# A two-layer hybrid trunk: the side steps' account, column strips and F32R logits

## The chip, the cores and the metric

The kernel runs on one core of a Trainium2 chip. The metric is the device time of one execution in microseconds (us): the median of several runs. Its engines are TensorE (PE in the profile; its weight loads are PEld), VectorE (DVE), ScalarE (ACT), GpSimd (POOL) and SyncE (SP).

## The reference, cut to what matters

Two layers over 256 tokens of width 2048. One input projection feeds four branches of width 512 (4 heads of 128): sparse attention with an indexer (A), retention (B), a gated linear recurrence (C) and attention into 256 memory tokens (M).

```python
def hybrid_layer(x, mem, ...):
    u = rms_norm(x, norm_g) @ w_in          # 2048 -> 15944 columns
    # A: rel = relu(q_idx . k_idx / 8); score = sum_h w_h rel_h; top 64 keys; softmax attention
    # B: rope(q), rope(k); (q . k) * decay; @ v; head norm
    # C: f = lb + (1 - lb) sigmoid(c_f); state = f * state + (1 - f) i; out = q . state; head norm
    # M: softmax(q . mk) @ mv, with mk, mv = mem @ w_mem_kv
    for n, (y, z) in enumerate(((y_a, a_z), (y_b, b_z), (y_c, c_z), (y_m, m_z))):
        merged = merged + sigmoid(gate_all[:, :, n]) * ((y * silu(z)) @ w_branch[n])
    return x + merged @ w_out
```

## The kernel before

**Products.** Weights stream from HBM in blocks of 512 rows by up to 512 columns (`gemm_plan`, `load`), four blocks ahead. Each half block is cut by `cut_piece` into a high part, a ScalarE copy to F32R (L247), and a low part, a VectorE subtraction (L248); four halves can be held (HL). `gemms` (L263) makes a product from three F32R matmuls (L286 to L288: high x high, high x low, low x high) for each 128 rows of the left side and each half of the tokens: twelve matmuls a half block, which leave the 256 tokens' results in PSUM. After each half block it calls `stream.pump` (L290), and then writes the next cut (L292).

**Side steps.** All that is not such a product (norms, rope, logits, softmax, the indexer's top-k, the recurrence's blocks, transposes) is written as Python generators, held as `Task` in `stream.tasks`. `pump` (L126) counts a tick (a half block of 512 columns is 1, narrower ones less) and steps the tasks in the order in which they were added, up to two steps (STEPS) a tick; a step that yields BLOCKED costs nothing. So each engine's instructions stand in an order that the program's writing fixes, and every engine runs its own in that order. `rest(n)` blocks a task until n ticks have gone by since it was reached; `bank` and `free` count two PSUM tiles for side products. `fold` transposes 32x32 blocks on VectorE and moves the blocks with 16 DMAs on POOL and SP, four a tick, then rests three ticks. `finish` (L136) is called where a product needs a task's result: it steps that task on with no product between, and counts ticks where nothing can move.

**The order of a layer.** Products: c_f and c_q, c_i, c_z, the indexer (256 and 328 columns), a_q, a_k, a_v, a_z, m_q, m_z, b_q, b_k, b_v, b_z; then four times, for branches C, A, M, B: the gate projection (8 ticks) and the branch product (2 ticks, L925), ahead of which `finish` takes the branch; then the output projection. Ahead of the first layer stand the memory's keys and values, whose left sides `memx` are split 8b - 4 ticks after the start (`split_later`).

**What the change touches.** `attend` (L426: logits at L439 in F32; memory without masks), `retention_scores` (L558: first key block at L562), `selection` (the indexer, L504: two heads side by side on rows 0 to 63 and 64 to 127), `hgrn_scores` (L652: groups of four column strips of 48 columns; L682: the last pair of levels, three strips of 96, 64 and 32 columns), `rope_t`, `branch_t` (transposes a branch and splits it, L303 and L304), `gate_path`. An F32 matmul of the program shows as two TensorE instructions.

Of the kernel before, what the change touches and what calls it, by code (L numbers as in the profile page):

```python
# [41 lines left out]
C_ID, C_D, C_COS, C_SIN, C_LEV = 0, 32, 32 + 1536, 32 + 1536 + 256, 32 + 1536 + 512  # L42
QUADS, FROM = (2, 8), (0, 1, 2, 0, 1, 0)
# [29 lines left out]
class Task:  # L73
    def __init__(self, steps):
        self.steps, self.done, self.value = steps, False, None

    def step(self):
        try:
            return next(self.steps) is not BLOCKED
        except StopIteration as e:  # L80
            self.done, self.value = True, e.value
            return True
# [7 lines left out]
GEN, HL, RAW = 18, 4, 4  # L90
MOVES, STEPS, BANKS, WARM = 4, 2, 2, 7


class Stream:
    def __init__(self):
        self.loaded = self.cut = self.used = self.ticks = self.idle = self.banks = 0
        self.owed = self.due = self.sent = 0
        self.raw, self.parts, self.tasks, self.moves = deque(), deque(), [], deque()
# [27 lines left out]
    def pump(self, part):  # L126
        self.tick(part)
        self.due = min(self.due + STEPS * part, STEPS)
        for t in list(self.tasks):
            if self.due < 1:  # L130
                break
            self.due -= t.step()
            if t.done:
                self.tasks.remove(t)
# [48 lines left out]
def trunk(ctx: ExitStack, tc: tile.TileContext, x, xt, memt, ng, qkg, hg, lbl, win, wmem, wbr, wout,  # L183
          cf, out):
    nc = tc.nc
    te, ve, ac, po, sy = nc.tensor, nc.vector, nc.scalar, nc.gpsimd, nc.sync
# [9 lines left out]
    def G(shape, name, dt=F32):  # L196
        return gen.tile(shape, dt, tag="g", name=name)
# [24 lines left out]
    stream = Stream()  # L222
# [23 lines left out]
    def cut_piece(hi, lo, r):  # L246
        ac.copy(hi, r)  # L247
        ve.tensor_sub(lo, r, hi.bitcast(F32))  # L248
# [110 lines left out]
    def transposed(src, name):  # L359
        u = yield from fold([((4, 2), src.rearrange("p t (h c) -> p h t c", h=4))], 8, name)  # L360
        return u.rearrange("p (h t) c -> p h (t c)", h=4)
# [12 lines left out]

    def normed_t(ps, rs, g, name):
        u = evac(ps, rs, name + "u")

        def turn():
            sq = G([128, 2, 512], name + "sq")
            ac.activation(sq, u, AF.Square)  # L380
            yield
            ss = SM(8, name + "ss")
            ve.reduce_sum(ss, sq.rearrange("p t (h d) -> p (t h) d", h=4), axis=AX.X)
            r = yield from rsq(ss, 8, 1.0 / HD, name)
            yield
            qn = u.rearrange("p t (h d) -> p (t h) d", h=4)
            ve.tensor_mul(qn, qn, bc(r, HD))
            yield
            pt = yield from transposed(u, name + "pt")
            ac.activation(pt, pt, AF.Copy, scale=g)  # L390
            return pt
        return turn()
# [10 lines left out]
    def branch_t(y, name):  # L403
        u = yield from transposed(y, name + "pt")
        return split(u, gen, "g", name)

    def head_norm(ps, zs, g, name):
        v = ps.rearrange("p (a d) -> p a d", a=8)
        zg = G([128, 2, 512], name + "zg")
        ve.tensor_tensor(zg, zs, g[:, None, :].to_broadcast([128, 2, W]), op=OP.mult)  # L410
        sq = G([128, 8, 128], name + "sq")
        ac.activation(sq, v, AF.Square)
        yield
        ss = SM(8, name + "ss")
        ve.reduce_sum(ss, sq, axis=AX.X)
        r = yield from rsq(ss, 8, 1.0 / HD, name)
        yield
        y1 = G([128, 8, 128], name + "y1")
        ve.tensor_mul(y1, v, bc(r, HD))
        stream.free()  # L420
        y = G([128, 2, 512], name + "y")
        ve.tensor_tensor(y, y1.rearrange("p (t h) d -> p t (h d)", t=2), zg, op=OP.mult)
        yield
        return (yield from branch_t(y, name))

    def attend(box, names, keys, name):  # L426
# [5 lines left out]
        y = G([128, 2, 512], name + "y")  # L432
        for t in range(2):
            nk = keys[t]
            nb = nk // 128
            yield from stream.bank()
            lg = PB(f"{name}lg{t}")[:, :4 * nk].rearrange("p (h s) -> p h s", h=4)
            for h in range(4):
                te.matmul(lg[:, h, :], qt[:, h, t * 128:t * 128 + 128], kt[:, h, :nk], start=True, stop=True)  # L439
# [13 lines left out]
            for h in range(4):  # L453
                ac.activation(p[:, h, :], lg[:, h, :], AF.Exp, bias=nm[:, h:h + 1], scale=ISQ,
                              accum_out=sm[:, h:h + 1])
            if masks is None:
                stream.free()
# [21 lines left out]
        return (yield from branch_t(y, name))  # L479

    def selection(qi0, qi1, name):
# [11 lines left out]
        for t in range(2):  # L493
# [3 lines left out]
            for g in range(8 // per):  # L497
# [3 lines left out]
                for h in range(g * per, g * per + per):  # L501
                    j = (h % 2) * (per // 2) + (h % per) // 2
                    q = slice((h % 2) * 64, (h % 2) * 64 + 64)
                    te.matmul(ps[:, j, :], qit[q, h // 2, t * 128:t * 128 + 128], kit[q, :nk],  # L504
                              start=True, stop=True)
# [20 lines left out]
    def rope_t(ps, rs, name):  # L526
        a = G([128, 2, 512], name + "a")
        b = G([128, 2, 512], name + "b")
        for t in range(2):
# [9 lines left out]
        ve.tensor_tensor(a, a, b, op=OP.add)  # L539

        def turn():
            yield
            return (yield from transposed(a, name + "pt"))
# [14 lines left out]
    def retention_scores(qt, kt, name):  # L558
        yield from stream.bank()
        p0 = PB(name + "s0").rearrange("p (h t) -> p h t", h=4)  # L560
        for h in range(4):
            te.matmul(p0[:, h, :], kt[:, h, 0:128], qt[:, h, :], start=True, stop=True)  # L562
# [13 lines left out]
    def hgrn_scores(uf, uq, lb, olb, name):  # L576
# [26 lines left out]

        strips = [slice(32 * i, 32 * i + 32) for i in range(4)]
# [75 lines left out]
        for g in range(8):  # L680
            for i, (c, w) in enumerate(((0, 96), (96, 64), (160, 32))):
                te.matmul(ps[strips[i], g, 128 - w:], kd[:, g // 2, (g % 2) * 128 + 32 * i:(g % 2) * 128 + 32 * i + 32],  # L682
                          vs[g // 4][:, g % 4, c:c + w], start=True, stop=True)
        for i, w in enumerate((96, 64, 32)):
            ac.copy(a[strips[i], :, 128 - w:], ps[strips[i], :, 128 - w:])
# [164 lines left out]
    for l in range(L):  # L850
# [8 lines left out]
        def mixed(scores, v, z, g, name):  # L859
            sc = yield from wait_for(box, key(scores))  # L860
            vt = yield from wait_for(box, key(v))
            zs = yield from wait_for(box, key(z))
            yield
            yield from stream.bank()
            return (yield from head_norm(mix_values(sc, vt, name), zs, g, name + "n"))
# [7 lines left out]
        early = []  # L873

# [12 lines left out]
        br[2] = stream.add(mixed("cs", "ci", "cz", hgs[:, 1, :], "c"))  # L887
# [8 lines left out]
        br[0] = stream.add(attend(box, [key(n) for n in ("aq", "ak", "av", "az", "ix")], (128, 256), "a"))  # L896
# [4 lines left out]
        br[3] = stream.add(attend(box, [key("mq"), f"mk{l}", f"mv{l}", key("mz"), None], (256, 256), "m"))  # L901
# [5 lines left out]
        br[1] = stream.add(mixed("bs", "bv", "bz", hgs[:, 0, :], "b"))  # L907
# [98 lines left out]
```

## Time and profile before

| | |
|---|---|
| median of 3 runs | 1866.32 us (1865.81 to 1867.09) |
| the profiled execution, its own time | 1866.38 us |
| its span, first to last instruction | 1864.4 us |
| instructions | 23441 |
| read from HBM | 353.60 MB |

The span lies 2.0 us below the profiled execution's own time. A busy time counts an instruction from its start to its end; matmuls overlap, so their pace is read from their starts.

### The profile page before, as it was taken

Reading aid. Unit: us, or ns where it says so; the run is one execution under the profiler, and the core shown is the slowest. Engines: PE = TensorE matmul, PEld = TensorE weight load, DVE = VectorE, ACT = ScalarE, POOL = GpSimd, SP = SyncE. Lnnn points to the kernel's source line nnn. Section 1 sums busy time; section 2 is a strip of 40 time slices with the busy share of each in tenths; the row PEclk is TensorE's granted clock in tenths of the full one; section 3 lists DMA queues with packets and bytes.
Section 4 is the critical chain, followed back from the end, with each engine's and each line's share of the span. In section 5 each row is a group of like instructions: output and inputs, shape, how many; then the busy total and the mean of one; then the engine's idle time right before and its main releaser. Section 6 shows DMA issues by size and latency. Waiting matters only on the chain.

```text
span 1864.4 us, 23441 instructions
## 1 busy us (share of the span) xinstructions
PE 1857.5 (100%) x8852; PEld 1548.7 (83%) x8852; DVE 1139.0 (61%) x1250; ACT 873.9 (47%) x1019; POOL 250.0 (13%) x405
## 2 busy tenths in 40 slices
PE   9999999999999999999999999999999999999999
PEld 7888888888888888888888888888888888888887
DVE  5655878675655555555566587867565555555554
ACT  5654554634444444444455454553444444444442
POOL 0022040241200000000021204024110000000000
PEclk9999999999999999999999999999999999999999
DMA  9775667686656565565686566668675656556563
GB/s 336 278 235 164 230 174 217 198 212 191 206 199 198 201 196 199 188 208 197 200 235 206 172 226 187 212 184 225 184 215 188 214 183 213 187 201 201 190 207 121
DMA packets 165952, 381.11 MB, mean 204 GB/s; under 512 B 111952, under 2 KB 112976, under 8 KB 125264
## 3 DMA queue, kind: packets, MB, share of 16 engines
q1 hardware_dynamic: 153408, 367.54, 60.8%
q0 software_dynamic: 12288, 11.95, 3.5%
q8 instruction: 69, 1.13, 0.2%
q14 instruction: 43, 0.35, 0.1%
q10 hardware_dynamic: 144, 0.13, 0.0%
HBM read 353.60 MB, written 2.10 MB: 191 GB/s over the span
## 4 chain that ended last, share of the span: by engine, by line
PE 99%; DMA 0%; DVE 0%; SPq 0%; ACT 0%; issue 0%
PE u L286 24%; PE u L287 24%; PE u L288 24%; PE wo L286 3%; PE wo L288 3%; PE bw L287 3%; PE bw L286 3%; PE bw L288 3%; PE wo L287 3%; PE mv L286 1%; PE mv L288 1%; PE mv L287 1%; PE mk L287 1%; PE mk L288 1%; PE mk L286 1%; PE mov L469 0%
## 5 line engine op out<-in xcount | busy, mean ns | idle before, releaser
L248 DVE TENSOR_TENSOR wlo<-raw,whi 128x1024 fp32r<-128x1024 f32 (+2 forms) x675 | 805.4, 1196 | 666.7 <-ACT whi L247 662.6
L247 ACT CAST whi<-raw 128x1024 fp32r<-128x1024 f32 (+2 forms) x675 | 696.0, 1032 | 918.1 <-PE u L288 697.3
L345 POOL DMA_DIRECT2D mgp<-mgpi x64 | 36.8, 583 | 797.8 <-ACT whi L247 589.8
L286 PE MATMUL u<-whi,x02h 128*128 128x512 f32 (+2 forms) x256 | 99.0, 387 | 0.0
L286 PE MATMUL u<-whi,x12h 128*128 128x512 f32 (+2 forms) x256 | 98.9, 387 | 0.0
L286 PE MATMUL u<-whi,x13h 128*128 128x512 f32 (+2 forms) x256 | 98.8, 386 | 0.0
L286 PE MATMUL u<-whi,x03h 128*128 128x512 f32 (+2 forms) x256 | 98.8, 386 | 0.0
L286 PE MATMUL u<-whi,x01h 128*128 128x512 f32 (+2 forms) x256 | 98.8, 386 | 0.0
L286 PE MATMUL u<-whi,x11h 128*128 128x512 f32 (+2 forms) x256 | 98.7, 386 | 0.0
L286 PE MATMUL u<-whi,x10h 128*128 128x512 f32 (+2 forms) x256 | 98.5, 385 | 0.0
L286 PE MATMUL u<-whi,x00h 128*128 128x512 f32 (+2 forms) x256 | 98.5, 385 | 0.0
L287 PE MATMUL u<-wlo,x02h 128*128 128x512 f32 (+2 forms) x256 | 98.2, 384 | 0.0
L287 PE MATMUL u<-wlo,x12h 128*128 128x512 f32 (+2 forms) x256 | 98.2, 384 | 0.0
L288 PE MATMUL u<-whi,x02l 128*128 128x512 f32 (+2 forms) x256 | 98.2, 384 | 0.0
L287 PE MATMUL u<-wlo,x03h 128*128 128x512 f32 (+2 forms) x256 | 98.2, 384 | 0.0
L287 PE MATMUL u<-wlo,x13h 128*128 128x512 f32 (+2 forms) x256 | 98.2, 384 | 0.0
L287 PE MATMUL u<-wlo,x11h 128*128 128x512 f32 (+2 forms) x256 | 98.2, 384 | 0.0
L287 PE MATMUL u<-wlo,x01h 128*128 128x512 f32 (+2 forms) x256 | 98.2, 384 | 0.0
L288 PE MATMUL u<-whi,x12l 128*128 128x512 f32 (+2 forms) x256 | 98.2, 384 | 0.0
L288 PE MATMUL u<-whi,x11l 128*128 128x512 f32 (+2 forms) x256 | 98.2, 384 | 0.0
L288 PE MATMUL u<-whi,x01l 128*128 128x512 f32 (+2 forms) x256 | 98.2, 384 | 0.0
L288 PE MATMUL u<-whi,x13l 128*128 128x512 f32 (+2 forms) x256 | 98.2, 384 | 0.0
(391 smaller groups left out, 3672.3 us busy)
## 6 DMA issues: line engine op xcount, KB each, us to landing
raw<-in_win SPq DMA_DIRECT2D x240, 1024.0 KB, 4.9
raw<-in_wbr SPq DMA_DIRECT2D x32, 1024.0 KB, 4.8
raw<-in_wout SPq DMA_DIRECT2D x32, 1024.0 KB, 4.8
raw<-in_wmem SPq DMA_DIRECT2D x12, 1024.0 KB, 5.2
raw<-in_win SPq DMA_DIRECT2D x8, 656.0 KB, 4.0
raw<-in_win SPq DMA_DIRECT2D x8, 512.0 KB, 4.0
raw<-in_wmem SPq DMA_DIRECT2D x5, 512.0 KB, 8.1
xr<-in_xt SPq DMA_DIRECT2D x4, 512.0 KB, 7.8
```

The lines of the kernel that those rows point to most:

```text
L247: ac.copy(hi, r)
L248: ve.tensor_sub(lo, r, hi.bitcast(F32))
L286: te.matmul(ps[t][:, u], ah[:, 2 * j + k, c], wh[:, k, u], start=first, stop=False)
L287: te.matmul(ps[t][:, u], ah[:, 2 * j + k, c], wl[:, k, u], start=False, stop=False)
L288: te.matmul(ps[t][:, u], al[:, 2 * j + k, c], wh[:, k, u], start=False, stop=last)
L345: q.dma_start(whole[b, :, a], inner[a, :, b])
```

## The change

**The account.** `Account` keeps a reckoned time for each engine; `Counted` and `Array` wrap the engines and add a formula's cost for each instruction written. `pump` stops stepping when VectorE or ScalarE are more than LATE (2500 ns) behind TensorE by it, and steps a task only when TensorE's time has reached the end of what the task's last step wrote, plus MARGIN (500 ns). **Later splits.** `branch_t` holds a branch's split until a given tick, counted from the tick at which the gates begin (`gates_at`). **F32R logits.** `halved` cuts an operand into two F32R halves (a ScalarE copy, a VectorE subtraction); `triple` makes a product of three F32R matmuls; memory logits and the retention's first block use it. **Strips.** The indexer's products go out as four strips of 32 output rows; the last pair's 96-wide piece is cut in 64 and 32, the latter on the fourth strip (`LAST`). Also: rope's second half of the tokens and its sum move into the task's steps, the exponentials are written in two steps, and GEN is 20 for 18.

```diff
@@ -40,6 +40,7 @@
...
 C_ID, C_D, C_COS, C_SIN, C_LEV = 0, 32, 32 + 1536, 32 + 1536 + 256, 32 + 1536 + 512
+LAST = ((0, 0, 0, 32, 64), (1, 1, 96, 64, 64), (2, 2, 160, 96, 32), (3, 0, 64, 96, 32))
 QUADS, FROM = (2, 8), (0, 1, 2, 0, 1, 0)
@@ -72,14 +73,76 @@
...
     def __init__(self, steps):
-        self.steps, self.done, self.value = steps, False, None
-
-    def step(self):
+        self.steps, self.done, self.value, self.ready = steps, False, None, 0.0
+    def step(self, account=None):
+        if account:
+            account.touched = 0.0
         try:
-            return next(self.steps) is not BLOCKED
+            moved = next(self.steps) is not BLOCKED
         except StopIteration as e:
-            self.done, self.value = True, e.value
-            return True
+            self.done, self.value, moved = True, e.value, True
+        if account and moved:
+            self.ready = account.touched + MARGIN
+        return moved
+class Account:
+    def __init__(self):
+        self.at, self.touched, self.table = dict(te=0.0, ve=0.0, ac=0.0, po=0.0), 0.0, None
+    def add(self, engine, cost, behind=()):
+        start = max([self.at["te"]] + [self.at[e] for e in behind] + [self.at[engine]])
+        self.at[engine] = start + cost
+        self.touched = max(self.touched, self.at[engine])
+    def late(self):
+        return max(self.at["ve"], self.at["ac"]) - self.at["te"]
+class Counted:
+    def __init__(self, engine, name, account):
+        self.engine, self.name, self.account = engine, name, account
+    def cost(self, op, args, kw):
+        n = max([int(np.prod(a.shape[1:])) for a in (*args, *kw.values()) if isinstance(a, bass.AP)] + [8])
+        if self.name == "po":
+            return 600 if op == "dma_start" else 1700 + n
+        if self.name == "ve":
+            return 155 + (1.4 if op == "copy_predicated" else 1.05) * n
+        func, table = kw.get("func", args[2] if op == "activation" and len(args) > 2 else None), 0
+        if func in (AF.Exp, AF.Sigmoid) and func != self.account.table:
+            self.account.table, table = func, 1300
+        return 215 + 0.8 * n + table + (200 if kw.get("accum_out") is not None else 0)
+    def __getattr__(self, op):
+        call = getattr(self.engine, op)
+        def counted(*args, **kw):
+            self.account.add(self.name, self.cost(op, args, kw))
+            return call(*args, **kw)
+        return counted
+class Array:
+    def __init__(self, engine, account):
+        self.engine, self.account = engine, account
+    def matmul(self, out, w, x, **kw):
+        n, k, m = int(np.prod(x.shape[1:])), w.shape[0], w.shape[1]
+        if x.dtype == F32R:
+            cost = (n + 32) / 2.4
+        else:
+            cost = (4 * n + 10) / 2.4 * (1.2 if k * m < 128 * 128 else 1.0) * k / 128 * m / 128
+        self.account.at["te"] += cost
+        self.account.touched = max(self.account.touched, self.account.at["te"])
+        return self.engine.matmul(out, w, x, **kw)
@@ -87,12 +150,14 @@
...
 HALVES = (slice(0, 256), slice(256, 512))
-GEN, HL, RAW = 18, 4, 4
+GEN, HL, RAW = 20, 4, 4
 MOVES, STEPS, BANKS, WARM = 4, 2, 2, 7
+MARGIN, LATE = 500.0, 2500.0
 class Stream:
-    def __init__(self):
+    def __init__(self, account):
+        self.account = account
         self.loaded = self.cut = self.used = self.ticks = self.idle = self.banks = 0
@@ -127,9 +192,10 @@
...
         for t in list(self.tasks):
-            if self.due < 1:
+            if self.due < 1 or self.account.late() > LATE:
                 break
-            self.due -= t.step()
+            if self.account.at["te"] >= t.ready:
+                self.due -= t.step(self.account)
             if t.done:
@@ -183,7 +249,9 @@
...
     nc = tc.nc
-    te, ve, ac, po, sy = nc.tensor, nc.vector, nc.scalar, nc.gpsimd, nc.sync
+    account = Account()
+    te, sy = Array(nc.tensor, account), nc.sync
+    ve, ac, po = (Counted(e, n, account) for e, n in ((nc.vector, "ve"), (nc.scalar, "ac"), (nc.gpsimd, "po")))
@@ -245,6 +313,7 @@
...
         ac.copy(hi, r)
+        account.at["ve"] = max(account.at["ve"], account.at["ac"])
         ve.tensor_sub(lo, r, hi.bitcast(F32))
@@ -372,6 +441,22 @@
...
+    def halved(src, name):
+        n = src.shape[2]
+        if n == 256:
+            hi, lo = G([128, 4, n], name + "hi", F32R), G([128, 4, n], name + "lo", F32R)
+        else:
+            both = G([128, 2, 4, n], name + "hl", F32R)
+            hi, lo = both[:, 0], both[:, 1]
+        ac.copy(hi, src)
+        yield
+        ve.tensor_sub(lo, src, hi.bitcast(F32))
+        return hi, lo
+    def triple(out, w, x):
+        for i, (a, b) in enumerate(((0, 0), (0, 1), (1, 0))):
+            te.matmul(out, w[a], x[b], start=i == 0, stop=i == 2)
@@ -400,11 +485,13 @@
...
-    def branch_t(y, name):
+    def branch_t(y, name, until):
         u = yield from transposed(y, name + "pt")
+        while stream.ticks < until:
+            yield BLOCKED
         return split(u, gen, "g", name)
-    def head_norm(ps, zs, g, name):
+    def head_norm(ps, zs, g, name, until):
         v = ps.rearrange("p (a d) -> p a d", a=8)
@@ -421,22 +508,31 @@
...
-        return (yield from branch_t(y, name))
-
-    def attend(box, names, keys, name):
+        return (yield from branch_t(y, name, until))
+    def attend(box, names, keys, name, until):
...
+        ks = None
...
+            if masks is None:
+                qs = yield from halved(qt[:, :, t * 128:t * 128 + 128], f"{name}q{t}")
+                if ks is None:
+                    ks = yield from halved(kt, name + "k")
+                yield from stream.rest(2)
...
-                te.matmul(lg[:, h, :], qt[:, h, t * 128:t * 128 + 128], kt[:, h, :nk], start=True, stop=True)
+                if masks is None:
+                    triple(lg[:, h, :], [u[:, h, :] for u in qs], [u[:, h, :] for u in ks])
+                else:
+                    te.matmul(lg[:, h, :], qt[:, h, t * 128:t * 128 + 128], kt[:, h, :nk], start=True, stop=True)
@@ -453,6 +549,8 @@
...
                               accum_out=sm[:, h:h + 1])
+                if h == 1:
+                    yield
             if masks is None:
@@ -476,7 +574,9 @@
...
         yield
-        return (yield from branch_t(y, name))
+        return (yield from branch_t(y, name, until))
+    strips = [slice(32 * i, 32 * i + 32) for i in range(4)]
@@ -498,11 +598,13 @@
...
                 ps = PB(f"{name}rp{t}{g}").rearrange("p (h s) -> p h s", h=per)
-                for h in range(g * per, g * per + per):
-                    j = (h % 2) * (per // 2) + (h % per) // 2
-                    q = slice((h % 2) * 64, (h % 2) * 64 + 64)
-                    te.matmul(ps[:, j, :], qit[q, h // 2, t * 128:t * 128 + 128], kit[q, :nk],
-                              start=True, stop=True)
+                for h in range(g * per, g * per + per, 2):
+                    for st in strips:
+                        for odd in range(2):
+                            q = slice(odd * 64, odd * 64 + 64)
+                            te.matmul(ps[st, odd * (per // 2) + (h % per) // 2, :],
+                                      qit[q, h // 2, t * 128 + st.start:t * 128 + st.stop], kit[q, :nk],
+                                      start=True, stop=True)
                 rl = G([128, per, nk], f"{name}rl{t}{g}")
@@ -526,7 +628,8 @@
...
         b = G([128, 2, 512], name + "b")
-        for t in range(2):
+        def rotate(t):
             pv = ps[:, t, :].rearrange("p (h d) -> p h d", h=4)
@@ -536,9 +639,13 @@
...
                                         st[:, :, lo:lo + 64], op0=OP.mult, op1=OP.mult)
-        ve.tensor_tensor(a, a, b, op=OP.add)
+        rotate(0)
         def turn():
+            rotate(1)
+            yield
+            ve.tensor_tensor(a, a, b, op=OP.add)
             yield
@@ -556,10 +663,13 @@
...
     def retention_scores(qt, kt, name):
+        ks = yield from halved(kt[:, :, 0:128], name + "k")
+        qs = yield from halved(qt, name + "q")
+        yield from stream.rest(2)
         yield from stream.bank()
...
         for h in range(4):
-            te.matmul(p0[:, h, :], kt[:, h, 0:128], qt[:, h, :], start=True, stop=True)
+            triple(p0[:, h, :], [u[:, h, :] for u in ks], [u[:, h, :] for u in qs])
         s0 = G([128, 4, 256], name + "s0s")
@@ -678,11 +786,11 @@
...
         for g in range(8):
-            for i, (c, w) in enumerate(((0, 96), (96, 64), (160, 32))):
-                te.matmul(ps[strips[i], g, 128 - w:], kd[:, g // 2, (g % 2) * 128 + 32 * i:(g % 2) * 128 + 32 * i + 32],
+            for to, i, c, t0, w in LAST:
+                te.matmul(ps[strips[to], g, t0:t0 + w], kd[:, g // 2, (g % 2) * 128 + 32 * i:(g % 2) * 128 + 32 * i + 32],
                           vs[g // 4][:, g % 4, c:c + w], start=True, stop=True)
-        for i, w in enumerate((96, 64, 32)):
-            ac.copy(a[strips[i], :, 128 - w:], ps[strips[i], :, 128 - w:])
+        for to, i, c, t0, w in LAST:
+            ac.copy(a[strips[i], :, t0:t0 + w], ps[strips[to], :, t0:t0 + w])
         stream.free()
@@ -856,13 +964,13 @@
...
-        def mixed(scores, v, z, g, name):
+        def mixed(scores, v, z, g, name, until):
             sc = yield from wait_for(box, key(scores))
...
             yield from stream.bank()
-            return (yield from head_norm(mix_values(sc, vt, name), zs, g, name + "n"))
+            return (yield from head_norm(mix_values(sc, vt, name), zs, g, name + "n", until))
@@ -871,6 +979,7 @@
...
         early = []
+        gates_at = stream.ticks + sum(n for c, n in CHUNKS[:16]) / 64
@@ -884,7 +993,7 @@
...
         stream.add(keep(key("cs"), hgrn_scores(uf, uq, lbv[:, l, :], olb[:, l, :], "c")))
-        br[2] = stream.add(mixed("cs", "ci", "cz", hgs[:, 1, :], "c"))
+        br[2] = stream.add(mixed("cs", "ci", "cz", hgs[:, 1, :], "c", gates_at - 2))
         box[key("ci")] = evac(proj(O_CI), rs, "ci")
@@ -893,18 +1002,18 @@
...
-        br[0] = stream.add(attend(box, [key(n) for n in ("aq", "ak", "av", "az", "ix")], (128, 256), "a"))
+        br[0] = stream.add(attend(box, [key(n) for n in ("aq", "ak", "av", "az", "ix")], (128, 256), "a", gates_at + 4))
...
-        br[3] = stream.add(attend(box, [key("mq"), f"mk{l}", f"mv{l}", key("mz"), None], (256, 256), "m"))
+        br[3] = stream.add(attend(box, [key("mq"), f"mk{l}", f"mv{l}", key("mz"), None], (256, 256), "m", gates_at + 12))
...
-        br[1] = stream.add(mixed("bs", "bv", "bz", hgs[:, 0, :], "b"))
+        br[1] = stream.add(mixed("bs", "bv", "bz", hgs[:, 0, :], "b", gates_at + 20))
...

```

## Rows read from the trace of the kernel before

**Rows 1.** The page's parts 1 (busy us, share, instructions) and 2 (granted clock).
```profile
PE 1857.5 (100%) x8852; PEld 1548.7 (83%) x8852; DVE 1139.0 (61%) x1250; ACT 873.9 (47%) x1019; POOL 250.0 (13%) x405
...
PEclk9999999999999999999999999999999999999999
```

**Rows 2.** TensorE's waits: who waited for whom, us in total, times, longest.
```profile
PE mk L286 <- ACT whi L247: 1.5, 1, 1.5
PE heat L709 <- DVE warm L706: 1.1, 1, 1.1
```

**Rows 3.** Timeline of TensorE, no side work: start us, us, engine, line, tiles, form.
```profile
900.02 0.39 PE L286 MATMUL wo<-whi,mg1h 128*128 128x512 f32 x1
...
902.74 0.39 PE L286 MATMUL wo<-whi,mg2h 128*128 128x512 f32 x1
```

**Rows 4.** Timeline of TensorE around a group of the memory logits.
```profile
370.13 0.39 PE L288 MATMUL u<-whi,x02l 128*128 128x512 f32 x1
370.36 1.89 PE L439 MATMUL mlg<-mk0pt,mqpt 128*128 128x256 f32 x8
371.90 0.58 PE L286 MATMUL u<-whi,x03h 128*128 128x512 f32 x1
372.31 0.40 PE L287 MATMUL u<-wlo,x03h 128*128 128x512 f32 x1
```

**Rows 5.** Timeline of TensorE in the 256-wide projection.
```profile
190.22 0.28 PE L288 MATMUL u<-whi,x02l 128*128 128x256 f32 x1
...
191.42 0.28 PE L286 MATMUL u<-whi,x03h 128*128 128x256 f32 x1
```

**Rows 6.** TensorE by line and form: count, busy us, mean ns, idle before.
```profile
L439 PE MATMUL mlg<-mk0pt,mqpt 128*128 128x256 f32 x16 | 3.8, 379 | 0.0
...
L562 PE MATMUL bs<-bqpt,bkpt 128*128 128x256 f32 x16 | 3.8, 379 | 0.0
...
L682 PE MATMUL cl<-cV,ck 128*32 128x96 f32 x32 | 3.0, 248 | 0.0
```

**Rows 7.** Timeline of TensorE around L682's group and the first of L652.
```profile
237.75 0.39 PE L288 MATMUL u<-whi,x00l 128*128 128x512 f32 x1
238.06 1.51 PE L682 MATMUL cl<-cV,ck 128*32 128x96 f32 x48
239.50 0.50 PE L286 MATMUL u<-whi,x01h 128*128 128x512 f32 x1
...
208.78 0.89 PE L652 MATMUL cl<-cV,ck 128*32 128x48 f32 x64
209.60 0.50 PE L286 MATMUL u<-whi,x00h 128*128 128x512 f32 x1
```

**Rows 8.** Timeline of TensorE around two of the indexer's groups.
```profile
270.52 1.16 PE L504 MATMUL ixrp<-ixkt,ixqt 64*128 64x128 f32 x16
271.62 0.50 PE L286 MATMUL u<-whi,x02h 128*128 128x512 f32 x1
...
296.32 1.13 PE L504 MATMUL ixrp<-ixkt,ixqt 64*128 64x256 f32 x8
297.39 0.50 PE L286 MATMUL u<-whi,x02h 128*128 128x512 f32 x1
```

**Rows 9.** Timelines of VectorE and of TensorE in the memory block.
```profile
42.69 1.22 DVE L304 TENSOR_TENSOR meml<-memr,memh 128x1024 fp32r<-128x1024 f32 x1
...
51.60 0.39 PE L288 MATMUL mk<-whi,meml 128*128 128x512 f32 x1
```

**Rows 10.** Timelines of VectorE and of TensorE after the rope of bq.
```profile
386.66 1.18 DVE L248 TENSOR_TENSOR wlo<-raw,whi 128x1024 fp32r<-128x1024 f32 x1
...
388.64 0.39 PE L287 MATMUL u<-wlo,x02h 128*128 128x512 f32 x1
```

**Rows 11.** Lines 303 and 922: count, ns min/median/max, first and last start.
```profile
L303 ACT CAST mh<-mpt x2: 1051/1052/1052, 502.7 to 1385.6; 128x1024 fp32r<-128x1024 f32 x2
...
L922 ACT ACTIVATE gate<-u,rs0r x32: 677/680/682, 478.2 to 886.8; 128x512 f32<-128x512 f32 x32
```

More of the change, by code (lines that the diff above doesn't have):

```diff
@@ L221, in trunk @@
     plan = gemm_plan(wmem, win, wbr, wout)
-    stream = Stream()
+    stream = Stream(account)
     def load(pieces=((0, 4),)):
@@ L602, in decayed @@
             return nt
-        strips = [slice(32 * i, 32 * i + 32) for i in range(4)]
         def eight(mask, *shape):
```

## The prediction

> **What bounds the kernel now.** I read the page's busy times first, then the waits of TensorE, then the timeline of single stretches. The page gives TensorE 1857.5 us of work in a span of 1864.4 us, and its granted clock is full in every slice; VectorE has 61% and ScalarE 47% [rows 1]. A modelled busy time can hide small gaps, so the waits and the starts have to agree with it. They do: the view has four waits of TensorE, all on the warm-up's line and on the first product's (mk), the longest two 1.5 and 1.1 us [rows 2]. In a stretch without side work twelve product steps of 128x512 start 2.72 us apart, 0.227 us each [rows 3]. I call these twelve steps, one half block of weights, a tick. So the span is a queue of TensorE work with no holes. Time can be gained only by work that TensorE no longer does, and lost only where a hole opens. SyncE's, VectorE's and ScalarE's time is worth nothing as long as it doesn't open one.
>
> **The logits in F32R** (`triple` in `attend` for memory and in `retention_scores` for the first key block). Today a group of four F32 products of 256 columns shows as eight instructions of TensorE. In the stretch of the memory logits the last product step ahead starts at 370.13 and the second one behind at 372.31, 2.18 us; two steps are 0.45, so the group costs 1.73 us [rows 4]. The new group has twelve F32R products of 256 columns. The half-width projection runs such products: ten of them start in 1.20 us, 0.12 us each [rows 5]. Twelve are 1.44 us, a gain of 0.29. The memory logits are four groups (two a layer: 16 instructions for one layer's keys) and the retention scores two (16 in both layers, same mean of 379 ns) [rows 6]: 6 x 0.29 = **1.74 us**. Bounds: if the long step behind the group (0.41 against 0.227) stayed, it would be 0.11 a group, 0.66 in all; more than 1.74 has no reason, since the QI steps already run without a gap.
> The new halves need ScalarE copies and VectorE subtractions: per layer two of 1024 elements and three of 512. At 1.22 us [rows 9] and 1.05 us [rows 11] for 1024 these are at most 6.1 and 5.3 us a layer, on engines with 39% and 53% idle. Cost on the path: zero, hidden under the products, because each triple rests two ticks (5.4 us) behind the last subtraction.
>
> **Four strips in the last pair.** The group of L682 runs three strips side by side, 96, 64 and 32 columns wide; from its first start to the next product step are 1.44 us. The group of L652, four strips of 48 columns, takes 0.82 us [rows 7]. With eight head groups and four passes of F32, the widest strip streams 8 x 4 x 96 = 3072 columns in the one and 1536 in the other: 0.62 us for 1536 columns, 0.40 ns a column. With 64 as the widest strip it is 2048 columns: 0.82 + 512 x 0.40 ns = 1.03 us, a gain of 0.41 a layer, **0.82 us**. Bounds: 0 (the fourth piece runs behind the first one in the same time as before) and 1.24 (as quick as L652). One more ScalarE copy a layer is hidden.
>
> **The indexer's strips.** Today two 64-row halves run side by side. The first query block has 16 instructions in 1.10 us from first start to the next product step, each part of the second 8 instructions in 1.07 us [rows 8]. Four pairs of 128 or two pairs of 256 are 2048 columns each, if the halves run side by side; by the line of L682 and L652 strips would take 1.03 us for as many columns. The gain is 0.07 twice and 0.04 four times, 0.30 at most. Eight pieces also start one after another, so I take **0.2 us**, between 0 and 0.30. No row has pieces that are cut in both directions; the loss if they don't run side by side is the second rival.
> A rule of the Trainium skill speaks against both edits on strips: TensorE: Matmul & The Clock Gate, section "Wait — 56ns, not 53.3ns?", says that starts of matmuls never come closer than about 25 ns. By it (an estimate from that page) the 64 instructions of the new L682 group and of the indexer's first block would take 1.6 us each, a loss. The trace differs: L652 starts 64 of them in 0.82 us, 13 ns each [rows 7]; I go by the row.
>
> **The account.** It adds no instruction. A pump now leaves off side steps when VectorE or ScalarE are over 2.5 us behind TensorE by its formulas, and a task waits until its own last step is reckoned done. TensorE waits for no weight today, so nothing can be won by it. The waits it adds are in the order of writing, not semaphores: behind a held step stand the later steps of its task alone, on SP and POOL its transposes' DMAs. Two places could lose.
> At the start its formulas put the first cuts' end at 9.4 us against 4.3 us of TensorE, so two pumps are held, and every `rest` counted from there begins two ticks later. The halves of the memory blocks feel this: the third block's was ready at 42.69 + 1.22 = 43.9 and is first read at 51.60 [rows 9], 7.7 us of cover. Two ticks take 5.4, 2.3 us are left: cost zero.
> The memory branch is the other: its first logits come 4 ticks later (two copies, two subtractions, the rest), the second ones 3 more, the split exponentials one each. That is 9 ticks, 24.5 us, if nothing is won back in the queue of transposing DMAs. Its last split starts at 502.7 and takes 2.3; it is read behind the third gate. The gates' first evaluation is at 478.2 [rows 11] and a gate with its branch product is ten ticks, so the third is at 478.2 + 2 x 27.2 = 532.6. The cover is 27.6 us: enough, but hardly. `until` delays the splits only to where they still lie 10 to 18 ticks ahead of use.
> Rope's second half, moved into a task, takes three VectorE operations and the sum out of the thickest VectorE burst. The cut at 386.66, 1.18 long, is read at 388.64 [rows 10], 0.8 us of cover, the least that I found; this gets better.
> GEN 20 for 18 covers the new tiles.
>
> **The sum.** 1.74 + 0.82 + 0.2 = 2.76 us. The profiled execution took 1866.38 us, its span and 2.0 us around it; the median of the three runs is 1866.32. So 1866.38 - 2.76 = **1863.6 us**, a span of 1861.6.
>
> **Rivals.**
> First, slower: the memory branch comes too late. `finish` then writes its remaining steps with no product between them and TensorE stands. It decides when the chain grows by over 27.6 us. With only the split left the price is 2.3 us a layer, net 1868.2; with a transpose's DMAs still out it is some 7.6 (a fold rests three ticks for them, so 5 to 8 us) a layer: 1863.6 + 15.2 = 1878.8. For it: 24.5 of 27.6 are used and two steps a tick are shared by all tasks. Against it: those ticks count no DMA queue time won back.
> Second: strips with 64 rows don't run side by side. If the two row halves follow each other, 2048 columns more a group, 6 x 0.82 = 4.9 us: 1863.8 + 4.9 = 1868.7. If each instruction took what the 64x128 ones take today (0.069 and 0.134 us), 64 and 32 of them would be 4.4 and 4.3 us a group, 3.3 more twice and 3.2 more four times, +19.5 us: 1883.3. Against it: L652's strips do run side by side, and so do today's halves. The chance below is for all prices of this kind, an instruction that costs more than its columns.
> The rule of the Trainium skill above (TensorE: Matmul & The Clock Gate, same section) is a mild case of it: by its 25 ns, an estimate, the two L682 groups and the indexer's two first blocks would lose 0.57 us each against my sum, 1865.9.
> Third: weights come late. The halves' operations fall on a burst: with 1.22 + 0.6 us more where the cover is 0.8, about 1 us a layer and place; two places, 4 us: 1867.6. Against it: the account holds steps exactly there. If the account held the start for four ticks instead of two, three splits would be 3.2 us late each: 1873.
> Fourth: more is gained (as quick as L652, the indexer too): 1.74 + 1.24 + 0.5 = 3.5 us, 1862.9, and something not seen: below 1862.6.
>
> **How the numbers follow.** A measurement of this kernel can tell about 0.2%, 3.7 us, from no change. Forecast (1862.6 to 1865): 0.74. Late branch 0.07, of which half is slower by over 0.2%. Strips one behind another 0.06, a third of it at the high price. Late weights 0.06, mostly within 0.2%. More gained 0.07, nearly all of it faster by over 0.2% only with the unseen part. So faster 0.08, same 0.86, slower 0.06. The range 1862.2 to 1866.6 takes in the forecast, most of the fourth and the light half of the third and, with a part of the first, about 8 in 10.
>
> **What would show it.** Right: waits of TensorE as today; twelve logits products 0.12 us apart with no long step behind; L682's group at 1.03 us; the indexer's at 1.03 to 1.10. Wrong: a wait of TensorE behind a cut, behind the memory branch's split near 530 or 1415 us, or in the first 80 us; indexer groups near 1.9 us or more.

## The result

The changed kernel takes 1878.98 us (median of 6 runs, 1877.67 to 1881.24) against 1866.34 us; the ratio is 1.0066, with a 95% interval of 1.0055 to 1.0077. Its profiled execution took 1878.08 us with a span of 1876.3 us, 11.9 us more than the span before. It is slower, where 1863.6 us and no measurable change were forecast.

The page's part 1 of the changed kernel answers to [rows 1]; part 2's clock line has one place that is no longer full:

```profile
PE 1856.5 (99%) x9100; PEld 1546.8 (82%) x9100; DVE 1148.5 (61%) x1260; ACT 886.5 (47%) x1035; POOL 250.0 (13%) x405
...
PEclk9999999999999999999999999999998999999999
```

TensorE's waits answer to [rows 2] (engine, tile and line, the releaser, then us in total, times, longest). All matmuls now have line 145, and the work of VectorE, ScalarE and GpSimd line 127, since the wrappers issue them; one goes by tiles.

```profile
PE bw L145 <- ACT mh L127: 12.0, 1, 12.0
PE mk L145 <- ACT whi L127: 2.5, 1, 2.5
PE heat L145 <- DVE warm L127: 1.1, 1, 1.1
```

One wait of 12.0 us is new: the branch product `bw` waits for `mh`, the high half of the memory branch's split. It happens once, in the second layer. Its place in the timeline, first TensorE's rows, then VectorE's and ScalarE's (start us, us, engine, line, operation, tiles, and in brackets the idle time ahead and who ended it):

```profile
1410.03 0.39 PE L145 MATMUL u<-whi,x13l 128*128 128x512 f32 x1
1410.26 1.95 PE L145 MATMUL mov<-mv,mpT 128*128 128x128 f32 x16
1424.21 0.79 PE L145 MATMUL bw<-whi,mh 128*128 128x512 f32 x1 [12.01 <-ACT mh L127]
1424.80 0.63 PE L145 MATMUL bw<-wlo,mh 128*128 128x512 f32 x1
...
1428.00 0.39 PE L145 MATMUL bw<-whi,ml 128*128 128x512 f32 x1
...
1412.67 0.68 DVE L127 TENSOR_TENSOR mon<-mov,mrc 128x512 f32<-128x512 f32 x1
1413.39 0.69 DVE L127 TENSOR_TENSOR my<-mon,mzzs 128x512 f32<-128x512 f32 x1
1414.12 1.25 DVE L127 STREAM_TRANSPOSE mpti<-my 128x1024 f32<-128x1024 f32 x1
1424.19 1.23 DVE L127 TENSOR_TENSOR ml<-mpt,mh 128x1024 fp32r<-128x1024 f32 x1 [8.83 <-ACT mh L127]
...
1423.12 1.04 ACT L127 CAST mh<-mpt 128x1024 fp32r<-128x1024 f32 x1 [10.45 <-DMA mpt<-mpti]
```

The memory branch's last products `mov` stand right behind the third gate's projection: `finish` wrote them, their evacuation, the transposes, the 16 DMAs and the split with no product between. TensorE waits for that whole chain at its real speed: 1.9 us of `mov`, 2.7 us of VectorE (1412.7 to 1415.4), 7.7 us of DMAs (to 1423.1) and the split. When it goes on, its steps are 0.4 to 0.7 us apart until 1427.8. The windows show why (per stretch: busy us of PE, PEld, DVE, ACT, POOL, granted clock, DMA share, GB/s):

```profile
1412.00:1424.00 12.00, 0.20 (x2) 0.01 (x1) 3.30 (x4) 1.55 (x3) 4.60 (x8) 0.73 0.54 131
1424.00:1426.00 2.00, 1.75 (x3) 1.01 (x4) 1.23 (x1) 0.16 (x1) 0.00 (x0) 0.50 0.00 0
1426.00:1428.00 2.00, 2.00 (x7) 1.53 (x5) 0.00 (x0) 0.00 (x0) 0.00 (x0) 0.56 0.00 0
```

During the wait the granted clock fell to the lower level, 1.2 GHz, and came back some 3.5 us after the products had begun again. Wait and slow steps together cost 14.1 us: from 1410.03 to 1428.00 are 17.97 us, in which nine steps of 0.227 and the group's usual 1.8 us were done.

The edits on TensorE's work did what was forecast. Timelines around one group of each kind, as in [rows 4], [rows 7] and [rows 8]:

```profile
381.00 0.39 PE L145 MATMUL u<-whi,x01l 128*128 128x512 f32 x1
381.22 0.28 PE L145 MATMUL mlg<-mkhi,mq0hl 128*128 128x256 f32 x1
...
382.66 0.40 PE L145 MATMUL u<-whi,x01h 128*128 128x512 f32 x1
382.89 0.40 PE L145 MATMUL u<-wlo,x01h 128*128 128x512 f32 x1
...
246.63 1.09 PE L145 MATMUL cl<-cV,ck 128*32 128x64 f32 x64
247.65 0.50 PE L145 MATMUL u<-whi,x02h 128*128 128x512 f32 x1
...
273.23 1.16 PE L145 MATMUL ixrp<-ixkt,ixqt 64*32 64x128 f32 x64
274.31 0.50 PE L145 MATMUL u<-whi,x02h 128*128 128x512 f32 x1
...
309.92 1.09 PE L145 MATMUL ixrp<-ixkt,ixqt 64*32 64x256 f32 x32
310.94 0.50 PE L145 MATMUL u<-whi,x01h 128*128 128x512 f32 x1
```

The twelve logits products take 1.44 us (381.22 to 382.66), and the step behind them is no longer late. The last pair takes 1.02 us for 1.44, the indexer's groups 1.08 for 1.10 and 1.02 for 1.07. So the account of the 11.9 us is: -2.8 from the edits, +14.1 from the stand, and some 0.6 of other differences. Most of these lie at the start: the third memory block's low half is first read at 52.04 us for 51.60 [rows 9], behind a wait for the first cut of 2.5 us for 1.5 (the last experiment shows that the start varies from execution to execution).

### The profile page after: what moved, and what is told of

Same layout as the page of the kernel before. It is cut to its first block, busy times and chain, and to the rows that moved or that the text cites. A ratio compares the mean times of both kernels' runs of the same rounds, so it can differ in the third digit from the quotient of the medians.

```text
span 1876.3 us, 23956 instructions
## 1 busy us (share of the span) xinstructions
PE 1856.5 (99%) x9100; PEld 1546.8 (82%) x9100; DVE 1148.5 (61%) x1260; ACT 886.5 (47%) x1035; POOL 250.0 (13%) x405
## 4 chain that ended last, share of the span: by engine, by line
PE 99%; DMA 0%; SPq 0%; DVE 0%; ACT 0%; issue 0%; ACTq 0%
PE u L145 73%; PE bw L145 9%; PE wo L145 9%; PE mv L145 2%; PE mk L145 2%; PE ixrp L145 0%; DMA raw<-in_wmem 0%; PE mlg L145 0%; PE bo L145 0%; PE co L145 0%; PE mov L145 0%; PE aov L145 0%; PE cl L145 0%; PE alg L145 0%; PE bs L145 0%; SPq L414 0%
## 5 line engine op out<-in xcount | busy, mean ns | idle before, releaser
L145 PE MATMUL u<-whi,x03l 128*128 128x512 f32 (+2 forms) x256 | 98.2, 383 | 0.0
L145 PE MATMUL u<-wlo,x10h 128*128 128x512 f32 (+2 forms) x256 | 98.1, 383 | 0.0
```

Of the source, the lines that this page charges most:

```text
L145: return self.engine.matmul(out, w, x, **kw)
```

## The experiments

**Theory A:** the account's holding makes the memory branch late, and `finish` then lets TensorE stand; the edits themselves are sound. **Rival B:** the memory branch's longer chain alone (two copies, two subtractions, a rest) makes it late. **Rival C:** the added VectorE and ScalarE work delays cuts. **Rival D**, for one run: the stand has nothing to do with when the branch is read. Each run's median stands beside the kernel before on the same chip: 1867.31 us for the first four, 1867.19 for the next four, 1868.56 (one execution) for the last two.

### The edits without the account

On the kernel before, core of the edit (the account, the later splits, the split exponentials and rope's steps are left out):

```diff
-GEN, HL, RAW = 18, 4, 4
+GEN, HL, RAW = 20, 4, 4
...
-                te.matmul(lg[:, h, :], qt[:, h, t * 128:t * 128 + 128], kt[:, h, :nk], start=True, stop=True)
+                if masks is None:
+                    triple(lg[:, h, :], [u[:, h, :] for u in qs], [u[:, h, :] for u in ks])
...
-            te.matmul(p0[:, h, :], kt[:, h, 0:128], qt[:, h, :], start=True, stop=True)
+            triple(p0[:, h, :], [u[:, h, :] for u in ks], [u[:, h, :] for u in qs])
...
+            for to, i, c, t0, w in LAST:
+                te.matmul(ps[strips[to], g, t0:t0 + w], kd[...], vs[g // 4][:, g % 4, c:c + w], start=True, stop=True)
```

> The kernel before with TensorE's three edits alone (F32R logits with their halves, four strips in the last pair, the indexer's strips, GEN 20) and without the account, the later splits, the split exponentials and rope's second half in steps. Theory A (the account's holding makes the memory branch late, the edits themselves are sound): no wait of TensorE for the memory branch's split in either layer, the groups at the costs that the changed kernel shows, so 1866.34 - 2.7 = 1863.6 us. Rival B (the memory branch's longer chain alone, two copies and two subtractions and a rest per query block, makes it late): a stand of about 12 us in at least one layer, 1875 us or more. Rival C (added VectorE and ScalarE work delays cuts once nothing holds it): waits of TensorE for weights, some us in total, 1865 to 1868.

Measured: 1864.74 us, ratio 0.9987 (0.9978 to 0.9996), 2.6 us faster. TensorE's waits are those of the start alone, for the warm-up's tile as before (1.1 us) and for the first cut:

```profile
PE mk L287 <- ACT whi L248: 2.4, 1, 2.4
```

The memory branch's split (tile `mh`: count, ns min/median/max, first and last start; the two starts are the two layers):

```profile
L304 ACT CAST mh<-mpt x2: 1052/1052/1053, 508.4 to 1389.9; 128x1024 fp32r<-128x1024 f32 x2
```

It starts 5.7 and 4.3 us later than before (502.7 and 1385.6 in [rows 11]), two ticks, and far ahead of its use. As A had it: against B (no stand) and against C (no wait for a cut). This version beats both kernels.

### The account without the edits

On the kernel before, core of the edit:

```diff
-            if self.due < 1:
+            if self.due < 1 or self.account.late() > LATE:
                 break
-            self.due -= t.step()
+            if self.account.at["te"] >= t.ready:
+                self.due -= t.step(self.account)
```

> The kernel before with the account alone: pump holds side steps by LATE and by MARGIN, nothing else is changed and TensorE's products are the old ones. Theory A: the memory branch is late in both layers, since nothing else (later splits, split exponentials, rope in steps) was suited to it; a stand of 6 to 12 us a layer, 1878 to 1890 us. Rival B: the chain has its old length, so no stand, 1866.3 us within 0.1%.

Measured: 1892.23 us, ratio 1.0135 (1.012 to 1.0151). No product of TensorE differs from the kernel before, and it is 24.9 us slower. Its waits:

```profile
PE bw L144 <- ACT mh L126: 19.8, 2, 10.2
```

Its memory split, by tile:

```profile
L126 ACT CAST mh<-mpt x2: 1044/1044/1045, 540.3 to 1435.6; 128x1024 fp32r<-128x1024 f32 x2
```

Both layers stand. The split starts 37.6 and 50.0 us later than before, with a chain of the old length. A holds, with a higher price than I had put (1878 to 1890); B's reading, no stand, is wrong.

### Nothing held

On the changed kernel:

```diff
-            if self.due < 1 or self.account.late() > LATE:
+            if self.due < 1:
                 break
-            if self.account.at["te"] >= t.ready:
-                self.due -= t.step(self.account)
+            self.due -= t.step(self.account)
```

> The changed kernel, but pump asks neither whether VectorE and ScalarE are late nor whether the task's last step is reckoned done; all else of the change stays. Theory A: the memory branch's last split comes some 9 ticks later than in the kernel before, just ahead of its use: no stand, 1863.6 us, at most 2 us more if the split's two instructions (2.3 us) are read at once. Rival B: late as in the changed kernel, 1875 to 1880 us. Rival C: waits for weights, 1865 to 1868 us.

Measured: 1865.44 us, ratio 0.999 (0.9981 to 0.9999), 1.9 us faster than before. There is no wait for the branch and none for a cut past the first one; the split starts at 515.9 and 1397.5. The waits (but for the warm-up's 1.1 us), and the split by tile:

```profile
PE mk L145 <- ACT whi L127: 1.9, 1, 1.9
```

```profile
L127 ACT CAST mh<-mpt x2: 1047/1048/1048, 515.9 to 1397.5; 128x1024 fp32r<-128x1024 f32 x2
```

That is 13.2 and 11.9 us later than before, five ticks and not nine. Undoing the two tests takes the whole loss away. The later splits (`until`) are no rival: they are in this run, which has no stand, and not in the second one, which has two.

### A wider limit

On the changed kernel:

```diff
-MARGIN, LATE = 500.0, 2500.0
+MARGIN, LATE = 500.0, 5000.0
```

> The changed kernel with one size changed: LATE 5000 for 2500 ns. Theory A: fewer steps are held, the branch comes in time, 1863.6 us and no stand. Rival B: 1875 to 1880 us. Rival C: the burst of VectorE work that the lower limit held back now delays a cut, with a wait of TensorE of 0.5 to 3 us behind a cut between 340 and 480 or 1220 and 1360 us.

Measured: 1865.36 us, ratio 0.999 (0.9982 to 0.9999). The branch comes in time (its split starts at 527.5 and 1405.7, the third gate's projection ends near 532 and 1415), so one size of the account, LATE, decides here. C's waits for cuts are not there, but another of 1.8 us is, which I had not named: in the second layer the memory's side product `mov` makes TensorE wait for transposing DMAs (the view names those of the sparse attention's tile `apT`).

```profile
1302.77 2.02 PE L145 MATMUL mov<-mv,mpT 128*128 128x128 f32 x16 [1.84 <-DMA apT<-apT1i]
```

### Each test alone

On the changed kernel, one test taken out at a time, one execution each. Without the LATE test:

```diff
-            if self.due < 1 or self.account.late() > LATE:
+            if self.due < 1:
```

> The changed kernel without the LATE test; MARGIN still holds a task until its last step is reckoned done. Theory A1 (LATE's break is what starves the memory branch): no stand, 1863 to 1867 us. Theory A2 (either test alone is enough, since both make the memory's steps wait behind the tasks ahead of it): a stand of 5 to 12 us in at least one layer, 1870 us or more.

Without the MARGIN test:

```diff
-            if self.account.at["te"] >= t.ready:
-                self.due -= t.step(self.account)
+            self.due -= t.step(self.account)
```

> The changed kernel without the MARGIN test; LATE at 2500 ns still ends a pump's steps. Theory A1: a stand as in the changed kernel, 1875 us or more. Theory A2: the same, in one layer or both. If there is no stand, 1863 to 1867 us, MARGIN is the cause and both are wrong.

Measured: 1879.75 us with MARGIN alone and 1892.57 with LATE alone. The wait for the branch with MARGIN alone, in the first layer:

```profile
PE bw L145 <- ACT mh L127: 11.3, 1, 11.3
```

With LATE alone, in both layers:

```profile
PE bw L145 <- ACT mh L127: 21.5, 2, 11.1
```

Either test is enough for a stand (A2). Taken together, as in the change, they let the first layer through (its split is at 520.8 us), which neither does alone. So a softer rule isn't always an earlier branch; that the order of writing, in which every held step has a part, makes the difference is my reading of the code, not tried.

### Memory logits back in F32, with the account

On the changed kernel, core of the edit:

```diff
-            if masks is None:
-                qs = yield from halved(qt[:, :, t * 128:t * 128 + 128], f"{name}q{t}")
-                if ks is None:
-                    ks = yield from halved(kt, name + "k")
-                yield from stream.rest(2)
...
-                if masks is None:
-                    triple(lg[:, h, :], [u[:, h, :] for u in qs], [u[:, h, :] for u in ks])
-                else:
-                    te.matmul(lg[:, h, :], qt[:, h, t * 128:t * 128 + 128], kt[:, h, :nk], start=True, stop=True)
+                te.matmul(lg[:, h, :], qt[:, h, t * 128:t * 128 + 128], kt[:, h, :nk], start=True, stop=True)
```

> The changed kernel with the memory logits back as four F32 matmuls, without their halves and rests; the account stays. The chain of the memory branch is 7 ticks shorter by the code. Theory A (the holding alone is enough): still a stand, 1866.3 - 1.6 + 5 to 12, 1870 us or more. Rival B (the longer chain is needed for it): no stand, 1866.3 - 1.6 = 1864.7 us.

Measured, in one execution: 1879.78 us. With a chain seven ticks shorter by the code the second layer still stands:

```profile
PE bw L145 <- ACT mh L127: 12.8, 1, 12.8
```

The longer chain is neither needed (here) nor enough (the first experiment). B falls.

### The memory branch read last

On the changed kernel:

```diff
-BR_ORDER = (2, 0, 3, 1)
+BR_ORDER = (2, 0, 1, 3)
...
-        br[3] = stream.add(attend(..., "m", gates_at + 12))
+        br[3] = stream.add(attend(..., "m", gates_at + 20))
...
-        br[1] = stream.add(mixed("bs", "bv", "bz", hgs[:, 0, :], "b", gates_at + 20))
+        br[1] = stream.add(mixed("bs", "bv", "bz", hgs[:, 0, :], "b", gates_at + 12))
```

> The changed kernel with branches taken in the order C, A, B, M in place of C, A, M, B (weights laid out alike), and the two branches' later splits exchanged: the memory branch is read 10 ticks (27 us) later, the retention branch 10 ticks earlier; nothing else. Theory A (a stand comes only where a branch is read ahead of its last split): the stand of 12 us shrinks to 4 us or less, and the retention branch, now due earlier, may cost up to 4 us: 1863.6 to 1871 us. Rival D (the stand has another cause, such as the split or the DMAs of the memory branch themselves): a stand of about 12 us, wherever the branch is read, 1876 us or more.

Measured: 1876.32 us, ratio 1.0047 (1.003 to 1.0064). The total is above the 1871 us that I gave A and lies where D's did; the waits tell them apart:

```profile
PE bw L145 <- ACT bnh L127: 3.2, 1, 3.2
PE bw L145 <- ACT mh L127: 3.2, 1, 3.2
...
PE bw L145 <- DVE ml L127: 0.5, 1, 0.5
PE bw L145 <- DVE bnl L127: 0.5, 1, 0.5
```

The 12 us are gone. In their place are two stands of 3.7 us, for the first layer's retention branch (now due earlier) and the second layer's memory branch, each for a split that was read at once. So the time of reading decides, against D. What I had too low is the price of a short stand. In the first layer the last step ahead of it starts at 532.81, and 25 steps later, at 544.06, the pace is back: 11.25 us for 5.67, a loss of 5.6 us, of which 3.7 are waits and 1.9 products at the lower clock:

```profile
537.00:539.00 2.00, 1.53 (x4) 1.12 (x4) 0.64 (x1) 0.00 (x0) 0.00 (x0) 0.50 0.88 344
539.00:541.00 2.00, 2.00 (x7) 1.53 (x7) 0.00 (x0) 0.00 (x0) 0.00 (x0) 0.65 0.32 135
```

Two of these and the edits' -2.8 are +8.4 us; +9.1 were measured.

### The first wait

The kernel before and the first experiment's kernel were run once more on one chip, to see the wait for the first full cut.

> The kernel before, once more, for its first waits alone: TensorE's wait for the first full cut was 1.5 us in its profile, 2.5 us in the changed kernel's and 1.1 to 2.7 in those of the experiments. If the arrival of the first weights varies from execution to execution, this one may show anything between 1.1 and 2.7 us; if the changes set it, 1.5 us.

> TensorE's edits alone, once more, for the same: 2.4 us were seen. If it varies from execution to execution, between 1.1 and 2.7 us; if the edits set it, 2.4 us.

Measured: 1867.55 and 1864.11 us. The wait in the kernel before:

```profile
PE mk L286 <- ACT whi L247: 1.2, 1, 1.2
```

In the edits alone:

```profile
PE mk L287 <- ACT whi L248: 1.0, 1, 1.0
```

The same programs had shown 1.5 and 2.4 us. The wait varies from execution to execution; the microsecond at the start of the changed kernel's profile can't be put down to the change. The granted clock behind it varies too. In the kernel before it was full in the first profile [rows 1]; in this one, behind a shorter wait, it was at the lower level for some microseconds, 0.74 on average from 10 to 15 us:

```profile
10.00:15.00 5.00, 5.00 (x18) 3.93 (x18) 3.33 (x6) 3.31 (x6) 0.00 (x0) 0.74 1.02 399
```

What the start costs shows in the last product of the memory's values, at 94.4 us in the kernel before and at 96.0 in the edits alone:

```profile
L288 PE MATMUL mv<-whi,meml x64: 388/389/390, 10.8 to 94.4; 128*128 128x512 f32 x64
L289 PE MATMUL mv<-whi,meml x64: 389/389/397, 12.4 to 96.0; 128*128 128x512 f32 x64
```

So the first experiment's profile lost 1.6 us there, and its span was still 1.1 us shorter (1863.3 for 1864.4): behind the start it gained 2.7 us, near the 2.8 that its groups add up to.

## Why the prediction was wrong

**The bound: right.** TensorE's queue has no holes but the one, and the span follows its holes and its products.

**The edits: right, term by term.** F32R logits 0.29 us a group as forecast (the step behind the group is not late), 1.74 in all. The last pair 0.42 for 0.41. The indexer's strips 0.02 and 0.05 for at most 0.07 and 0.04, in all 0.24 for 0.2 (one group of each kind read, times their number); pieces cut in both directions do run side by side. The sum of 2.8 us is borne out by the first experiment as a whole, 2.6 us with an interval of 0.7 to 4.1. The Trainium skill's floor (TensorE: Matmul & The Clock Gate, section "Wait — 56ns, not 53.3ns?") would have made the groups of 64 instructions 1.6 us each, an estimate from its 25 ns. The trace disagrees: the 64 instructions of the last pair take 1.02 and those of the indexer's first block 1.08, so for pieces side by side the row decides again.

**The hidden work: right.** No run shows a wait for a cut past the first 15 us, with the account or without.

**The account's start: right.** In the changed kernel the third memory block's low half is ready at 48.57 + 1.22 = 49.8 us and first read at 52.04, 2.2 us of cover where 2.3 were forecast.

```profile
48.57 1.22 DVE L127 TENSOR_TENSOR meml<-memr,memh 128x1024 fp32r<-128x1024 f32 x1
...
52.04 0.39 PE L145 MATMUL mk<-whi,meml 128*128 128x512 f32 x1
```

**The memory branch's chain: the step that failed.** I counted nine ticks from the code, 24.5 us, against 27.6 us of cover, and wrote "enough, but hardly". The nine ticks were those of the longer chain alone, and they were too many: without the account it is two (first experiment) or, with the rest of the change (third experiment), five. The cover was a microsecond shorter than I put it (the branch's first read in the kernel before is at 531.5 us, not 532.6); that decides nothing. What I left out is the holding itself, to which I gave no price. I had written that behind a held step "stand the later steps of its task alone", and I put no tick on it. By the code more stands behind it: the memory's task comes after the sparse attention's in the list, two steps a tick are shared, a pump that LATE breaks off leaves the tasks at the end unstepped, and MARGIN makes each step of a long chain wait for the one before. In the second layer of the changed kernel the copy of the first query half starts at 1269.3 and the last subtraction of the keys at 1286.9; with nothing held they are at 1255.9 and 1264.2. The last products `mov` start at 1411.9 for 1369.0. The changed kernel, by tile (first and last start):

```profile
L127 ACT CAST mq0hl<-mqpt x2: 619/619/619, 370.1 to 1269.3; 128x512 fp32r<-128x512 f32 x2
L127 DVE TENSOR_TENSOR mklo<-mk1pt,mkhi x1: 1219/1219/1219, 1286.9 to 1286.9; 128x1024 fp32r<-128x1024 f32 x1
L145 PE MATMUL mov<-mv,mpT x64: 270/275/275, 426.1 to 1411.9; 128*128 128x128 f32 x64
```

The third experiment's:

```profile
L127 ACT CAST mq0hl<-mqpt x2: 603/603/603, 374.4 to 1255.9; 128x512 fp32r<-128x512 f32 x2
L127 DVE TENSOR_TENSOR mklo<-mk1pt,mkhi x1: 1184/1184/1184, 1264.2 to 1264.2; 128x1024 fp32r<-128x1024 f32 x1
L145 PE MATMUL mov<-mv,mpT x64: 270/275/276, 428.5 to 1369.0; 128*128 128x128 f32 x64
```

The first and the last of these four operations (copy and subtraction of the queries, then of the keys) start 17.6 us apart in place of 8.3. So the holding puts the branch 13.4 us behind the third experiment at the first copy, 22.7 at the last subtraction and 42.9 at `mov`; there `finish` takes over, and the way from `mov` to the split takes 11.2 us where it takes 28.5 among products. The split is at 1423.1 us, 37.5 us later than before, over the cover of 27.6: 11.9 of these are there with nothing held, 25.6 come with the holding. In the first layer it is at 520.8, 18.1 us later, and in time. The two layers differ in the order in which the held steps go out: in the first the memory's first logits (381.2 us) come ahead of the sparse attention's second ones (391.8), in the second behind them (1292.6 and 1263.7). Whether this order makes the difference, and which held step makes the order, was not tried and stays open.

**The rival's price: too low.** The first rival named the mechanism, its place near 1415 us and 1868.2 to 1878.8 us, and got a chance of 0.07. It took some 7.6 us a layer in both layers; there was a stand in one, and it cost 14.1. That its upper price of 1878.8 lies next to the measured 1878.98 is luck. The chain was further back than I priced (not only the DMAs and the split were left, but the last products and their evacuation), and the clock's fall, 2.1 us beside the wait's 12.0, was not in it.

**The cover that the account was to protect.** The least cover of a cut was 0.8 us, behind the rope burst [rows 10]. Nothing was read late there before, so there was nothing to win, as forecast. Without any holding the third experiment has no wait for a later cut either.

## What to carry to other kernels

Where one engine is the bound and never waits, a rule that holds other work back has no wait to win and may make one; ask of each held step by when its result is read, and count the waiting in the list, not only the steps of its chain. A forced finish costs the whole remaining chain at its real speed and the clock on top, so a margin of one tenth is no margin. When a change brings sound edits and a new scheduler together, try them apart: the edits alone gave 2.6 us here, the scheduler alone took 24.9.

## What the runs showed of the hardware

Behind a wait of 3.2 us and one of 0.5 the granted clock was 0.50, the lower of its two levels (1.2 GHz), and this short stand of 3.7 us cost 5.6. The length of a wait alone does not tell whether the clock falls: at the start it stayed full behind 2.5 us in the changed kernel, and fell behind 1.2 us in the kernel before, run again.

A group of F32 products left the next F32R step late (0.41 us for 0.227, [rows 4]); the group of F32R products did not (382.66 to 382.89 us). Pieces of 64 rows by 32 columns run side by side: 64 instructions in 1.08 us, which the trace of before could not show.
